# GpSimd computes the low halves of its weights in operations of 256 columns instead of 1024

## The chip, the cores and the metric

The kernel runs on one core of one Trainium2 chip. The core has five engines with queues of their own: TensorE (PE in the rows; its weight loads are listed apart as PEld), VectorE (DVE), ScalarE (ACT), GpSimd (POOL) and SyncE (SP, which here only issues transfers). Each engine takes its instructions in a fixed order, and waits between engines are semaphores. The metric is device time in microseconds (us), lower is better; it is the median of three runs.

## The reference, cut to what matters

Two transformer-like blocks run on 256 positions of width 2048, all in float32. The first has attention, a pooling branch and a feed-forward part with a short convolution; the second works on 272 positions (16 more in front) and has a state-space scan with a second, 31-tap convolution, and then a neighbourhood attention. Nearly all arithmetic is in products of activations with large weight matrices:

```python
proj = h @ w_in[l]                                        # 2048 x 4096
x = x + jnp.concatenate([a, m], axis=-1) @ w_out[l]       # 2048 x 2048
u = h @ w_up                                              # 2048 x 11264
return (jax.nn.silu(gate) * val) @ w_down                 # 5632 x 2048
proj = jnp.einsum("bld,de->ble", u, w_in)                 # even layer: 2048 x 12352
h + jnp.einsum("ble,ed->bld", jnp.concatenate([y_a, y_b], axis=-1), w_out)   # 4096 x 2048
proj = jnp.einsum("bld,de->ble", u, w_in)                 # odd layer: 2048 x 8192
```

## The kernel before

**Products in three parts.** To keep float32 accuracy with TensorE's faster fp32r operands, every operand is split into a high part, which is the value rounded to fp32r, and a low part, which is the value minus the high part. A product is then three matmuls per 128 rows of depth: `wh*xh` (L226), `wh*xl` (L227) and `wl*xh` (L228), all added in one PSUM tile `acc`. The function is `products`; `rows` (L239 to L241) is a variant with the operands' roles exchanged, used for the first block's q, k and v.

**Chunks and pieces.** Weights come in chunks of 128 output columns, in the order that `plan` writes down: a `raw` tile of 128 partitions by up to 2048 columns, that is, 16 blocks of depth 128 side by side. Three `raw` buffers are loaded ahead by SP (L165). `split_next` splits a chunk in pieces of 8 blocks (1024 columns). For each piece ScalarE writes the high part, `wH` (L185), and VectorE or GpSimd subtracts it from the weights to get the low part, `wL` (L186). Both have four buffers, so two chunks. A chunk of the feed-forward's second matrix (`down`) has 11 blocks: one piece of 1024 columns and one of 384.

**Who splits.** The table `POOL` names for each kind of chunk how many of its pieces go to GpSimd: one of two for most, both for `B`, `C` and `xs` (the inputs of the scan), none for `k` and `q` but one piece of each of the first chunks. VectorE does the rest. `chunk` calls `split_next` for the next chunk before the current chunk's matmuls are written, so a chunk is split while the one before it is multiplied. The first three chunks are already split in operations of a quarter piece (`step = n // 4`, 256 columns).

**What else these engines do.** VectorE takes the products out of PSUM, adds and scales, splits activations (`split_act`, `xl` at L265 and L268), does the convolutions' taps (L666, L770, with a PSUM tile as input and output), and the scan's element-wise work (`e`, `A`, `z`, `u`: L857, L865, L866, L810, L914). ScalarE does the high parts, activations and copies out of PSUM. GpSimd does little but its low parts.

**The order** on each engine is that of the program text, as the tile framework lays it out. The places spoken of below: the mixing step of the pooling branch (`pooled`, `mix`; about 164 to 227 us from the span's start), the scan (`meta_set`, `heads`, `pair`; 1460 to 1660 us), and the second half of the even layer's output projection (chunks `e_out` with half 0; 1810 to 1916 us). In that last loop each of the 16 outputs `t` is scaled, added and reordered on VectorE (L1006 to L1009), stored by ScalarE's queue (L357), and split for the next layer (L267, L268).

Of the kernel before, what the change touches and what calls it, by code (L numbers as in the profile page):

```python
# [10 lines left out]
F32 = mybir.dt.float32  # L11
F32R = mybir.dt.float32r
AF = mybir.ActivationFunctionType
OP = mybir.AluOpType
# [43 lines left out]
class Kernel:  # L58
# [112 lines left out]
    def split_next(self):  # L171

        nc = self.nc
        key = self.order[self.n_split][0]
        raw, kt, pieces = self.wt[self.n_split]
        k0 = len(pieces) * self.PIECE
        n = min(self.PIECE, kt - k0) * P
        w = raw[:, k0 * P:k0 * P + n]
        H = self.wp.tile([P, self.PIECE * P], F32R, name="wH", tag="wH", bufs=self.PIECES)
        L = self.wp.tile([P, self.PIECE * P], F32R, name="wL", tag="wL", bufs=self.PIECES)  # L180
        eng = nc.gpsimd if self.on_pool(key, len(pieces)) else nc.vector
        step = n // 4 if self.n_split < 3 else n
        for o in range(0, n, step):
            c = slice(o, o + step)
            nc.scalar.activation(H[:, c], w[:, c], AF.Copy)  # L185
            eng.tensor_tensor(L[:, c], w[:, c], H[:, c].bitcast(F32), op=OP.subtract)  # L186
        pieces.append((H, L))
        if k0 * P + n == kt * P:
            self.n_split += 1
# [1080 lines left out]
```

## Time and profile before

| what | us |
|---|---|
| median of 3 runs | 2448.98 (2447.66 to 2449.26) |
| profiled execution, its own time | 2449.59 |
| its span, first to last instruction | 2447.8 |
| PE busy in it | 2410.7 (98%) |
| DVE busy | 1639.5 (67%) |
| ACT busy | 1308.1 (53%) |
| POOL busy | 1046.8 (43%) |

A busy time is the union of an engine's instructions. The mean of one matmul (286 ns) is its length from entry to end; as matmuls overlap, one enters every 0.12 us. "Idle before" is the time that an engine stood still before an instruction, with the instruction that let it go on. The span is cut into windows where a stage is of interest; PEclk in a window is the share of TensorE's full clock that was granted in it.

### The profile page before, as it was taken

What the parts mean: (1) busy time and instruction counts of PE and PEld (TensorE: products, weight loads), DVE (VectorE), ACT (ScalarE), POOL (GpSimd) and SP (SyncE); (2) the same over time, 40 slices, a digit from 0 to 9 for tenths busy, and PEclk for the clock granted to TensorE, in tenths of its full rate; (3) what the DMA queues carried; (4) which work ended last, traced back from release to release, by engine and by line L of the source; (5) the groups of instructions that cost most, each with busy time, mean ns of one, the idle gap of its engine ahead of it and who ended that gap; (6) DMA issues with size and microseconds to landing.
All of it is one profiled execution on the core that took longest, in us unless ns stands there. A gap on an engine that the chain in (4) does not pass through costs nothing.

```text
span 2447.8 us, 48352 instructions
## 1 busy us (share of the span) xinstructions
PE 2410.7 (98%) x19718; PEld 2373.6 (97%) x19718; DVE 1639.5 (67%) x2770; ACT 1308.1 (53%) x2125; POOL 1046.8 (43%) x441
## 2 busy tenths in 40 slices
PE   8999999999999999999999999999999999999998
PEld 8998999999999999999999998889999999999998
DVE  6566456666666666779999988798767544444433
ACT  6564455554454454553547766775544444445553
POOL 1133444445445545654458863323434333333443
PEclk9999999999999999999999999999999999999999
DMA  8545655556756756875455555555676544445553
GB/s 283 184 146 181 235 193 184 188 184 205 234 188 200 243 181 197 256 230 180 163 193 187 189 169 198 180 181 168 224 236 203 183 159 172 158 171 182 187 190 121
DMA packets 116415, 471.47 MB, mean 193 GB/s; under 512 B 17376, under 2 KB 54496, under 8 KB 72416
## 3 DMA queue, kind: packets, MB, share of 16 engines
q1 hardware_dynamic: 94880, 443.87, 53.6%
q10 hardware_dynamic: 21312, 24.52, 2.8%
q8 instruction: 154, 2.52, 0.4%
q14 instruction: 69, 0.57, 0.1%
HBM read 448.79 MB, written 19.54 MB: 191 GB/s over the span
## 4 chain that ended last, share of the span: by engine, by line
PE 90%; DVE 3%; issue 2%; ACT 2%; DMA 1%; SPq 0%; POOL 0%; ACTq 0%; POOLq 0%; DVEq 0%
PE acc L226 27%; PE acc L227 27%; PE acc L228 27%; PE acc L241 2%; PE acc L239 2%; PE acc L240 2%; ACT wH L185 1%; PE cvp L1078 1%; PE gp L1068 1%; DVE wL L186 1%; DVE win L513 1%; PE gp L1044 1%; PE cvp L888 0%; DVE e L865 0%; ACT e L849 0%
## 5 line engine op out<-in xcount | busy, mean ns | idle before, releaser
L226 PE MATMUL acc<-xh,wH 128*128 128x256 f32 (+1 forms) x5856 | 1675.1, 286 | 9.4 <-ACT xh L267 6.2
L227 PE MATMUL acc<-xl,wH 128*128 128x256 f32 (+1 forms) x5856 | 1670.4, 285 | 0.0
L228 PE MATMUL acc<-xh,wL 128*128 128x256 f32 (+1 forms) x5856 | 1667.2, 285 | 0.4
L186 POOL TENSOR_TENSOR wL<-raw,wH 128x1024 fp32r<-128x1024 f32 (+1 forms) x435 | 1042.5, 2399 | 1382.3 <-ACT wH L185 1282.5
L185 ACT ACTIVATE wH<-raw 128x1024 fp32r<-128x1024 f32 (+1 forms) x838 | 832.0, 998 | 790.8 <-PE acc L227 589.4
L226 PEld LDWEIGHTS acc<-xh,wH 128*128 128x128 f32 x5856 | 1108.5, 189 | 17.6 <-ACT xh L267 6.6
L228 PEld LDWEIGHTS acc<-xh,wL 128*128 128x128 f32 x5856 | 1107.7, 189 | 1.5 <-POOL wL L186 1.0
L227 PEld LDWEIGHTS acc<-xl,wH 128*128 128x128 f32 x5856 | 1107.6, 189 | 1.5 <-issue 0.8
L186 DVE TENSOR_TENSOR wL<-raw,wH 128x1024 fp32r<-128x1024 f32 (+2 forms) x403 | 582.0, 1446 | 144.4 <-ACT wH L185 139.0
L666 DVE SCALAR_TENSOR_TENSOR cvp<-u,prm,cvp 128x264 f32<-128x264 f32 (+14 forms) x480 | 211.0, 489 | 1.4 <-ACT cvp L660 0.7
L265 DVE TENSOR_TENSOR xl<-y,xh 128x256 fp32r<-128x256 f32 x44 | 98.7, 2243 | 25.1 <-ACT xh L264 25.1
L239 PE MATMUL acc<-wH,xh 128*128 128x256 f32 x384 | 109.2, 286 | 6.0 <-ACT xh L267 6.0
L590 DVE TENSOR_TENSOR u<-acc,r 128x256 f32<-128x256 f32 x88 | 36.7, 418 | 110.6 <-PE acc L228 108.5
L241 PE MATMUL acc<-wH,xl 128*128 128x256 f32 x384 | 109.0, 285 | 0.7 <-DVE xl L268 0.6
L240 PE MATMUL acc<-wL,xh 128*128 128x256 f32 x384 | 107.9, 283 | 0.0
L239 PEld LDWEIGHTS acc<-wH,xh 128*128 128x128 f32 x384 | 73.1, 191 | 6.2 <-ACT xh L267 6.1
L291 DVE TENSOR_TENSOR nacc<-nacc,sq 128x272 f32<-128x272 f32 (+1 forms) x103 | 68.2, 662 | 10.4 <-ACT sq L280 9.2
L241 PEld LDWEIGHTS acc<-wH,xl 128*128 128x128 f32 x384 | 73.2, 191 | 1.6 <-DVE xl L268 1.5
L240 PEld LDWEIGHTS acc<-wL,xh 128*128 128x128 f32 x384 | 72.9, 191 | 0.1
L770 DVE SCALAR_TENSOR_TENSOR gp<-c,prm,gp 128x270 f32<-128x270 f32 (+1 forms) x128 | 63.8, 498 | 5.7 <-ACT gp L766 5.3
L622 DVE TENSOR_TENSOR xw<-acc,xw 128x256 f32<-128x256 f32 x64 | 27.2, 425 | 51.6 <-PE acc L228 48.2
L592 ACT ACTIVATE y<-u,prm 128x256 f32<-128x256 f32 x88 | 52.2, 594 | 14.9 <-DVE u L590 14.7
(227 smaller groups left out, 1416.5 us busy)
## 6 DMA issues: line engine op xcount, KB each, us to landing
raw<-in_e_w_in_dram SPq DMA_DIRECT2D x97, 1024.0 KB
raw<-in_w_up_dram SPq DMA_DIRECT2D x88, 1024.0 KB
raw<-in_o_w_in_dram SPq DMA_DIRECT2D x64, 1024.0 KB
raw<-in_w_down_dram SPq DMA_DIRECT2D x64, 704.0 KB
raw<-in_e_w_out_dram SPq DMA_DIRECT2D x32, 1024.0 KB
raw<-in_w_qkv_dram SPq DMA_DIRECT2D x21, 1024.0 KB
raw<-in_w_out_dram SPq DMA_DIRECT2D x16, 1024.0 KB
raw<-in_o_w_out_dram SPq DMA_DIRECT2D x16, 1024.0 KB
```

The costliest lines, as they stand in the source:

```text
L185: nc.scalar.activation(H[:, c], w[:, c], AF.Copy)
L186: eng.tensor_tensor(L[:, c], w[:, c], H[:, c].bitcast(F32), op=OP.subtract)
L226: nc.tensor.matmul(ps, wh, xh, start=k == 0, stop=False)
L227: nc.tensor.matmul(ps, wh, xl, start=False, stop=False)
L228: nc.tensor.matmul(ps, wl, xh, start=False, stop=k == n - 1)
L239: nc.tensor.matmul(ps[b], xh, H[:, o:o + 256], start=k == 0, stop=False)
L240: nc.tensor.matmul(ps[b], xh, L[:, o:o + 256], start=False, stop=False)
L241: nc.tensor.matmul(ps[b], xl, H[:, o:o + 256], start=False, stop=k == 15)
L265: nc.vector.tensor_tensor(l, x, h.bitcast(F32), op=OP.subtract)
L291: nc.vector.tensor_tensor(st["acc"], st["acc"], sq, op=OP.add)
L666: nc.vector.scalar_tensor_tensor(cps[i][:, a:b], u[i][:, a + s:b + s], self.prm_("dww", k * 16 + i), cps[i][:, a:b], op0=OP.mult, op1=OP.add)
L770: nc.vector.scalar_tensor_tensor(y[:, a:b], t[:, a + d:b + d], self.prm_("ecw", k * 32 + c), y[:, a:b], op0=OP.mult, op1=OP.add)
```

## The change

The subtraction that makes `wL` is written in operations of at most 256 columns where GpSimd does it. Where VectorE does it, and in ScalarE's `wH`, nothing is changed.

```diff
         eng = nc.gpsimd if self.on_pool(key, len(pieces)) else nc.vector
         step = n // 4 if self.n_split < 3 else n
+
+        sub = 256 if eng is nc.gpsimd else step
         for o in range(0, n, step):
             c = slice(o, o + step)
             nc.scalar.activation(H[:, c], w[:, c], AF.Copy)
-            eng.tensor_tensor(L[:, c], w[:, c], H[:, c].bitcast(F32), op=OP.subtract)
+            for i in range(o, o + step, sub):
+                c = slice(i, min(i + sub, o + step))
+                eng.tensor_tensor(L[:, c], w[:, c], H[:, c].bitcast(F32), op=OP.subtract)
```

GpSimd's 427 operations of 1024 columns become 1708 of 256; its 8 operations of the first chunks are as they were. On the other four engines no instruction is moved, added or removed. What stands differently is what they wait for. GpSimd's queue in the second half of the output projection (`e_out`), before:

```order
L186 TENSOR_TENSOR wL<-raw,wH 128x1024 [waits DMAHW3_49,PE_49,Activation_49]
L186 TENSOR_TENSOR wL<-raw,wH 128x1024 [waits DMAHW6_49,PE_49,Activation_49]
L186 TENSOR_TENSOR wL<-raw,wH 128x1024 [waits DMAHW1_49,PE_49,Activation_49]
L186 TENSOR_TENSOR wL<-raw,wH 128x1024 [waits DMAHW4_49,PE_49,Activation_49]
L186 TENSOR_TENSOR wL<-raw,wH 128x1024 [waits DMAHW7_49,PE_49,Activation_49]
```

GpSimd's queue there, with the change (L190 is L186 of before):

```order
L190 TENSOR_TENSOR wL<-raw,wH 128x256 [waits DMAHW3_49,PE_49,Activation_49]
L190 TENSOR_TENSOR wL<-raw,wH 128x256 x3
L190 TENSOR_TENSOR wL<-raw,wH 128x256 [waits DMAHW6_49,PE_49,Activation_49]
L190 TENSOR_TENSOR wL<-raw,wH 128x256 x3
L190 TENSOR_TENSOR wL<-raw,wH 128x256 [waits DMAHW1_49,PE_49,Activation_49]
L190 TENSOR_TENSOR wL<-raw,wH 128x256 x3
```

Each piece is now four operations; the first carries the waits (for the load, for TensorE to be done with the buffer, and for ScalarE's high part), and the three behind it carry none.

TensorE's queue at a chunk of the same stage, the first piece, before:

```order
L226 MATMUL acc<-xh,wH 128x272 [waits Activation_49]
L227 MATMUL acc<-xl,wH 128x272
L228 MATMUL acc<-xh,wL 128x272 [waits Pool_49]
L226 MATMUL acc<-xh,wH 128x272
L227 MATMUL acc<-xl,wH 128x272
L228 MATMUL acc<-xh,wL 128x272
L226 MATMUL acc<-xh,wH 128x272
L227 MATMUL acc<-xl,wH 128x272
L228 MATMUL acc<-xh,wL 128x272
```

TensorE's queue there, with the change (L230 to L232 are L226 to L228 of before):

```order
L230 MATMUL acc<-xh,wH 128x272 [waits Activation_49]
L231 MATMUL acc<-xl,wH 128x272
L232 MATMUL acc<-xh,wL 128x272 [waits Pool_49]
L230 MATMUL acc<-xh,wH 128x272
L231 MATMUL acc<-xl,wH 128x272
L232 MATMUL acc<-xh,wL 128x272
L230 MATMUL acc<-xh,wH 128x272
L231 MATMUL acc<-xl,wH 128x272
L232 MATMUL acc<-xh,wL 128x272 [waits Pool_49]
```

The matmuls stand where they stood. Each quarter of a GpSimd piece now has a wait of its own, in front of every second `wl*xh` matmul, where one wait for the whole piece stood at its first; that is 1277 waits more.

## Rows read from the trace of the kernel before

**Rows 1.** The page's first part: busy time of each engine over the span.
```profile
PE 2410.7 (98%) x19718; PEld 2373.6 (97%) x19718; DVE 1639.5 (67%) x2770; ACT 1308.1 (53%) x2125; POOL 1046.8 (43%) x441
```

**Rows 2.** PE's waits, 190 to 230 us: for whom, us in total, times, longest.
```profile
PE acc L226 <- ACT xh L267: 2.9, 1, 2.9
PE acc L226 <- DVE xl L268: 2.6, 2, 2.1
```

**Rows 3.** PE's waits, 1400 to 1700 us.
```profile
PE gp L817 <- DVE mu L905: 4.4, 1, 4.4
PE cvp L894 <- DVE xl L265: 4.0, 3, 3.2
```

**Rows 4.** PE's waits, 1900 to 1920 us.
```profile
PE acc L226 <- ACT xh L267: 3.4, 1, 3.4
```

**Rows 5.** Windows: length, busy PE, PEld, DVE, ACT, POOL, then PEclk, DMA, GB/s.
```profile
198.50:205.30 6.80, 5.08 (x24) 5.08 (x25) 4.92 (x13) 1.90 (x4) 0.47 (x1) 0.50 0.27 77
...
1478.50:1482.00 3.50, 3.50 (x15) 2.69 (x16) 3.50 (x10) 2.14 (x6) 0.00 (x0) 0.51 0.51 157
1557.00:1563.80 6.80, 6.41 (x23) 5.58 (x24) 3.69 (x9) 4.27 (x9) 0.00 (x0) 0.50 0.87 294
1642.40:1645.80 3.40, 3.40 (x17) 3.40 (x16) 3.40 (x3) 1.16 (x2) 2.84 (x1) 0.50 0.88 304
...
1915.40:1922.20 6.80, 6.01 (x23) 5.53 (x24) 4.59 (x5) 2.85 (x4) 2.36 (x1) 0.50 0.69 194
```

**Rows 6.** Line L186, both engines: count, shortest/median/longest in ns, first and last start.
```profile
L186 POOL TENSOR_TENSOR wL<-raw,wH x435: 755/2402/4750, 9.8 to 2422.9; 128x1024 fp32r<-128x1024 f32 x142, 128x256 fp32r<-128x256 f32 x3
L186 DVE TENSOR_TENSOR wL<-raw,wH x403: 409/1225/2893, 5.1 to 2425.6; 128x1024 fp32r<-128x1024 f32 x107, 128x384 fp32r<-128x384 f32 x22, 128x256 fp32r<-128x256 f32 x6
```

**Rows 7.** Timeline, one turn of the `e_out` loop: start, us, engine, line, operation, [idle before].
```profile
1883.78 0.52 ACT L267 ACTIVATE xh<-xw,prm 128x272 fp32r<-128x272 f32 x1 [3.62 <-DVE xw L1009]
...
1885.65 2.62 POOL L186 TENSOR_TENSOR wL<-raw,wH 128x1024 fp32r<-128x1024 f32 x1 [3.76 <-ACT wH L185]
...
1886.55 2.81 DVE L186 TENSOR_TENSOR wL<-raw,wH 128x1024 fp32r<-128x1024 f32 x1 [0.54 <-ACT wH L185]
...
1889.36 0.39 DVE L1009 COPY xw<-eo 128x256 f32<-128x256 f32 x1
...
1890.18 0.52 ACT L267 ACTIVATE xh<-xw,prm 128x272 fp32r<-128x272 f32 x1 [3.66 <-DVE xw L1009]
```

**Rows 8.** Timeline of DVE in the pooling branch: two held operations and a free one.
```profile
170.90 2.38 DVE L520 TENSOR_TENSOR mix<-mix,p 128x16 f32<-128x16 f32 x1
...
192.93 0.42 DVE L513 TENSOR_TENSOR win<-win 128x252 f32<-128x252 f32 x1
...
197.11 2.14 DVE L513 TENSOR_TENSOR win<-p 128x255 f32<-128x255 f32 x1
```

**Rows 9.** Timeline, operations of GpSimd back to back, and a DVE operation among them.
```profile
1268.05 7.36 POOL L186 TENSOR_TENSOR wL<-raw,wH 128x1024 fp32r<-128x1024 f32 x3
...
1270.70 2.44 DVE L745 TENSOR_TENSOR u<-u,sig 128x272 f32<-128x272 f32 x1
```

**Rows 10.** Timeline of the first chunks: four 256-column operations on GpSimd, DVE beside them.
```profile
15.47 3.59 POOL L186 TENSOR_TENSOR wL<-raw,wH 128x256 fp32r<-128x256 f32 x4 [2.31 <-ACT wH L185]
...
17.51 1.82 DVE L268 SCALAR_TENSOR_TENSOR xl<-xin,prm,xh 128x256 fp32r<-128x256 f32 x2
```

**Rows 11.** Timeline in the scan: one kind of DVE operation free and held, GpSimd's beside it.
```profile
1545.89 1.49 DVE L914 TENSOR_TENSOR u<-u,r 128x272 f32<-128x272 f32 x4
...
1546.16 4.75 POOL L186 TENSOR_TENSOR wL<-raw,wH 128x1024 fp32r<-128x1024 f32 x1 [6.85 <-ACT wH L185]
...
1548.91 5.90 DVE L914 TENSOR_TENSOR u<-u,r 128x272 f32<-128x272 f32 x5
```

**Rows 12.** Window in the stage with both pieces on GpSimd; columns as in rows 5.
```profile
1300.00:1400.00 100.00, 100.00 (x800) 99.78 (x799) 91.56 (x226) 78.06 (x116) 81.24 (x35) 1.00 0.54 187
```

**Rows 13.** The page's groups: weight loads of `wL`, busy, mean ns, idle before.
```profile
L228 PEld LDWEIGHTS acc<-xh,wL 128*128 128x128 f32 x5856 | 1107.7, 189 | 1.5 <-POOL wL L186 1.0
```

## The prediction

> **What bounds the kernel now.** I read the busy times first: PE is busy for 2410.7 of the span's 2447.8 us, POOL for 1046.8 [rows 1]. POOL's own length is therefore not the question. What the change can reach is where PE stands still, or runs at half its clock after it stood still, and what it must not do is to make POOL late for PE.
>
> PE's waits gather in three places. In the mixing step of the pooling branch PE waits 2.9 us for `xh` and 2.6 us for `xl` [rows 2]; in the scan 4.4 us for `mu` and 4.0 us for `xl`, both from DVE [rows 3]; at the end of the first half of `e_out`'s second loop 3.4 us for `xh` [rows 4]. After each, a window has the granted clock at 0.50, the lower level of 1.2 GHz [rows 5]. What PE did there at half speed is lost by half: 5.08 / 2 = 2.5 us after the mixing step, (3.50 + 6.41 + 3.40) / 2 = 6.7 us in the scan, 6.01 / 2 = 3.0 us after `e_out`. Together 2.9 + 2.6 + 2.5 = 8.0, 4.4 + 4.0 + 6.7 = 15.1 and 3.4 + 3.0 = 6.4 us, that is 29.5 us.
>
> Then I asked why DVE is late at these places, and the timelines answer. DVE's low part of 1024 columns takes 1.22 us in the middle, 2.89 at most [rows 6]. In each turn of the `e_out` loop it takes 2.81 us: it starts 0.90 us after a POOL operation of 2.62 us, and ends 1.09 us behind that one's end, about its own length [rows 7]. So it does nothing until POOL is done: it is held. The same shows in the pooling branch, where an operation on 128x16 takes 2.38 us, and one on 255 columns 2.14 us, where its free sister needs 0.42 [rows 8], and in the scan, where four `u` operations take 1.49 us when free and five take 5.90 beside POOL [rows 11]. All these DVE operations read two SBUF tiles. It goes the other way too: POOL's 4.75 us [rows 11] contain the time in which DVE's run of `u` operations stood ahead of it.
>
> **The change, part by part.**
>
> *A piece on POOL gets longer.* One of 1024 columns takes 2.40 us in the middle, one of 256 columns 0.755 at the shortest [rows 6]. Four make 3.02 us if nothing disturbs them, 3.59 where DVE got between them [rows 10]. I take 3.02, since in the stage where it matters (below) DVE has few such operations, and keep 3.59 for the range. The 427 pieces cost POOL 427 x 0.62 = 265 us, which by itself is free: POOL is idle for 57% of the span.
>
> *Where POOL has both pieces* (`B`, `C`, `xs`; 32 chunks, 64 pieces) it is 81% busy, and PE does 800 matmuls in 100 us [rows 12], 0.125 us each, so a piece's 24 matmuls take 3.00 us. A piece of 3.02 is behind by 0.02 x 64 = 1.3 us over the stage. Against that stands what the finer waits give: a quarter releases its own two blocks, so PE can begin on a piece 2.40 - 0.755 = 1.64 us earlier than now. 1.64 is over 1.3: I cost this at nothing. The cover is gone above 3.00 + 1.64 / 64 = 3.03 us a piece.
>
> *PE's 1277 new waits.* The weight loads of `wL` carry the old ones; 5856 of them show 1.5 us of idle time before them in all [rows 13]. If every new wait cost what these loads cost on average, 1277 x 1.5 / 5856 = 0.3 us. I take 0; above, 0.3; below zero there is nothing to win, since nothing waits there.
>
> *The hold gets shorter.* A DVE operation that comes while POOL works now waits for the rest of an operation of up to 2.40 us, afterwards for the rest of one of 0.755, if DVE gets its turn between two POOL operations. It does: three POOL operations back to back last 7.36 us, and DVE's `u` (L745), which started within the second, took 2.44 us and so ended before the third was over [rows 9]; among the 256-column operations of the first chunks two DVE operations take 0.91 us each [rows 10], not the rest of the piece. Against the trace stands a rule of the Trainium skill: GPSIMD Engine Reference, 2.1 Instruction dispatch, says that the completion of an operation does not hold back the next Pool instruction, and that each of GpSimd's cores goes on to it as soon as its share is done. By that rule a gap between quarters need not exist, and the sum below would turn into the third rival's; the rows just named show a turn at the seam, so I go by them.
>
> - `e_out`: the turn is 1890.18 - 1883.78 = 6.40 us [rows 7], against PE's 48 matmuls x 0.125 = 6.00. DVE's `wL` is in the chain of that turn, directly ahead of `xw` (L1009) and `xh` [rows 7]. It arrives 0.90 us into the piece, so in the second quarter, and waits until 2 x 0.755 = 1.51: held 0.61 instead of 2.62 - 0.90 = 1.72. The turn would be 6.40 - 1.11 = 5.29 us, under PE's 6.00. PE becomes the bound of this loop, and 0.40 us saved per turn would already do. Gain: the whole 6.4 us (bounds 0 and 6.4).
> - The mixing step: five holds lie in its chain, from the first to the third row of [rows 8], together about 9.65 us over free durations (2.38 and 2.14 are the first and the last). At one quarter each, 5 x 0.755 = 3.8 stay, so up to 5.9 us of the chain go. But DVE runs almost without gaps there, and may meet two quarters of one piece. I take 5 of the 8.0 us (bounds 0 and 8.0).
> - The scan: the five `u` operations of [rows 11] are held 5.90 - 5 x 0.37 = 4.0 us by two pieces; with quarters 1.5 stay, so 2.5 go, from the wait of 4.0 or from its half clock. I put the same 2.5 on the wait of 4.4, whose chain has two POOL pieces beside it too, and 1.0 on the last window of half clock. That is 6 of 15.1 us (bounds 0 and 15.1); the rest is DVE's and ACT's own work.
>
> Sum: 6.4 + 5 + 6 = 17.4 us off the profiled execution's 2449.59, that is 2432.2. The profiled time is 0.6 above the median of 2448.98, so I say **2432**.
>
> **The rivals.**
>
> 1. *Holds are shared out anew.* Between two DVE operations of a run POOL gets its next quarter, so a run of four meets four holds of 0.755, 3.0 us in place of 2.0. The two slow operations in a row at 17.51 [rows 10] speak for this; against it speaks the run of four free ones ahead of POOL's late one [rows 11]. Then mixing and scan give nothing, and in `e_out` the copy L1009 meets the third quarter: 1.11 - 0.755 = 0.36 of the 0.40 us per turn are won, some 4 us of 6.4 at most. That is 2445.6 or more; about **2447**, no change that could be told.
> 2. *POOL becomes the bound in `B`, `C`, `xs`* (slower). At 3.59 us a piece, PE would wait 64 x (3.59 - 3.00) - 1.6 = 36 us; with the 17.4 us won elsewhere that is 2449.6 - 17.4 + 36 = **2468**. It costs from 3.03 us a piece, and decides the sign from 3.00 + (17.4 + 1.6) / 64 = 3.30. For it: 3.59 is the only row of four quarters in a row. Against it: DVE's operations beside those four read two SBUF tiles at each output, those in this stage mostly come from PSUM.
> 3. *GpSimd does not let go between quarters* (slower). A hold is then up to 3.02 us in place of 2.40. `e_out`: 15 turns x 0.62 = 9.3 us more; mixing 5 x 0.62 = 3.1; scan 4 x 0.62 = 2.5: 2449.6 + 14.9 = **2464.5**. This is the time by the page named above; [rows 9, 10] speak against it.
> 4. *All of it goes.* PE finds its operands ready at all three places: 2449.6 - 29.5 = **2420**. Against it: the scan's chains hold much work of DVE and ACT that no POOL operation touches.
>
> That the change does not do what it says is excluded: the order shows four operations for one, and the waits by quarter.
>
> **How the numbers follow.** Forecast (2424 to 2441) 0.54; all of it goes 0.16; shared out anew 0.16; POOL the bound 0.08; never lets go 0.06. A measurement of this kernel can tell a difference of about 0.2%, 4.9 us. So: faster 0.54 + 0.16 = 0.70, the same 0.16, slower 0.14. The range takes in the forecast's bounds, all of the fourth rival and most of the first: 2418 to 2449; the slower cases stay outside it.
>
> **What would show it.** In the `e_out` loop DVE's `wL` at about 1.8 us instead of 2.81, the turn at 6.0, and PE's wait of 3.4 us with the half clock behind it gone: right for `e_out`. The 255-column operations of the mixing step at 0.4 to 1.2 us, and waits there below 3 us: right for the holds. POOL's 256-column operations at 0.70 to 0.76 us and no wait of PE for POOL between 1265 and 1455 us: right for the stage with both pieces. Wrong would be: DVE's `wL` in `e_out` above 2.8 us (third rival); PE waiting for `wL` of POOL again and again while both pieces are POOL's (second); as many us of held DVE operations in the mixing step and the scan as now, in smaller portions (first).

## The result, and the profile after

The changed kernel takes 2417.15 us (median; 2416.74 to 2419.06) against 2449.12 for the kernel before beside it: a ratio of 0.9871, with a 95% interval of 0.9857 to 0.9886. That is 32 us faster, where 17 were forecast, and it lies 0.9 us below the range.

The profiled execution took 2416.97 us, its span 2415.2. The first row of its page answers to [rows 1]; the second is GpSimd's low parts and the third the weight loads of `wL` (as [rows 13]; line, operation, count, busy us, mean ns, idle before).

```profile
PE 2396.5 (99%) x19718; PEld 2363.3 (98%) x19718; DVE 1464.8 (61%) x2770; ACT 1304.1 (54%) x2125; POOL 1340.5 (56%) x1722
...
L190 POOL TENSOR_TENSOR wL<-raw,wH 128x256 fp32r<-128x256 f32 x1716 | 1336.2, 810 | 1056.4 <-ACT wH L187 1046.4
...
L232 PEld LDWEIGHTS acc<-xh,wL 128*128 128x128 f32 x5856 | 1103.2, 188 | 0.2
```

POOL is busy for 294 us more than before and nobody is late for it: the loads of `wL`, with 1277 waits more, show 0.2 us of idle time in all. DVE, whose instructions are the same, is busy for 175 us less. That is time in which it stood held with an operation begun.

PE's waits in the changed kernel, over the whole span (us in total, times, longest), which answer to [rows 2 to 4]:

```profile
PE acc L243 <- ACT xh L271: 5.8, 1, 5.8
PE cvp L898 <- DVE xl L269: 0.8, 2, 0.6
PE acc L230 <- DVE xl L272: 0.8, 1, 0.8
PE gp L342 <- ACT rs L335: 0.7, 1, 0.7
PE acc L245 <- DVE xl L272: 0.6, 1, 0.6
PE acc L230 <- ACT xh L271: 0.5, 1, 0.5
PE gp L821 <- DVE mu L909: 0.2, 1, 0.2
PE gp L330 <- ACT sq L284: 0.2, 1, 0.2
```

The first is the kernel's very start, which has nothing to do with the change. The wait of 4.4 us for `mu` is 0.2, the 4.0 for `xl` in the scan 0.8, the 3.4 at the end of `e_out` is gone. With them went the half clock: these windows lie where those of [rows 5] lay (same columns; PEclk is the number after POOL's).

```profile
198.00:205.00 7.00, 7.00 (x62) 7.00 (x61) 4.12 (x7) 2.72 (x4) 2.81 (x4) 1.00 0.45 152
...
1466.00:1473.00 7.00, 7.00 (x58) 7.00 (x58) 7.00 (x16) 4.26 (x9) 3.28 (x4) 1.00 0.57 193
1538.00:1545.00 7.00, 7.00 (x54) 6.23 (x51) 3.72 (x8) 5.13 (x10) 4.60 (x4) 1.00 0.74 236
1886.00:1893.00 7.00, 7.00 (x56) 6.92 (x56) 4.97 (x6) 3.47 (x5) 5.08 (x6) 1.00 0.63 189
```

PE runs the same matmuls in the same order in both kernels, so the start of one matmul in the two traces tells where the time went:

| stage | start of the same matmul before, after (us) | ahead | won in the stage |
|---|---|---|---|
| ahead of the mixing step's waits | 194.1, 193.4 | 0.7 | 0.7 |
| behind the mixing step | 226.9, 218.9 | 8.0 | 7.3 |
| ahead of the scan's first wait | 1455.0, 1446.6 | 8.4 | 0.4 |
| behind the scan | 1651.8, 1626.9 | 25.0 | 16.6 |
| behind `e_out` | 1921.2, 1889.0 | 32.2 | 7.2 |
| end of the span | 2447.8, 2415.2 | 32.6 | 0.4 |

The three places that the prediction named give 31.1 of the 32.6 us; what was wrong is how much each gives. The 0.7 us of the first row are there at 20 us already and are not the change's: the traces of the eleven other kernels whose first three chunks are split alike stand there between 0.2 us behind the kernel before and 1.1 ahead of it. A difference of two traces below 1 us says little.

### The profile page after: what moved, and what is told of

It is laid out like the page before. It is cut to its first block, busy times and chain, and to the rows that moved or that the text cites. A ratio compares the mean times of both kernels' runs of the same rounds, so it can differ in the third digit from the quotient of the medians.

```text
span 2415.2 us, 49918 instructions
## 1 busy us (share of the span) xinstructions
PE 2396.5 (99%) x19718; PEld 2363.3 (98%) x19718; DVE 1464.8 (61%) x2770; ACT 1304.1 (54%) x2125; POOL 1340.5 (56%) x1722
## 4 chain that ended last, share of the span: by engine, by line
PE 96%; DVE 1%; issue 1%; ACT 1%; DMA 1%; POOL 0%; SPq 0%; POOLq 0%; ACTq 0%
PE acc L230 29%; PE acc L231 29%; PE acc L232 29%; PE acc L245 2%; PE acc L243 2%; PE acc L244 2%; PE cvp L1082 1%; PE gp L1072 1%; PE gp L1048 1%; PE cvp L892 0%; PE cvp L898 0%; DVE e L870 0%; PE gp L1042 0%; ACT wH L187 0%; POOL wL L190 0%
## 5 line engine op out<-in xcount | busy, mean ns | idle before, releaser
L190 POOL TENSOR_TENSOR wL<-raw,wH 128x256 fp32r<-128x256 f32 x1716 | 1336.2, 810 | 1056.4 <-ACT wH L187 1046.4
L230 PE MATMUL acc<-xh,wH 128*128 128x256 f32 (+1 forms) x5856 | 1670.1, 285 | 1.3 <-DVE xl L272 0.8
L232 PE MATMUL acc<-xh,wL 128*128 128x256 f32 (+1 forms) x5856 | 1662.6, 284 | 0.0
L230 PEld LDWEIGHTS acc<-xh,wH 128*128 128x128 f32 x5856 | 1104.0, 189 | 9.0 <-issue 3.3
L232 PEld LDWEIGHTS acc<-xh,wL 128*128 128x128 f32 x5856 | 1103.2, 188 | 0.2
L190 DVE TENSOR_TENSOR wL<-raw,wH 128x1024 fp32r<-128x1024 f32 (+2 forms) x403 | 477.5, 1187 | 154.9 <-ACT wH L187 145.8
L295 DVE TENSOR_TENSOR nacc<-nacc,sq 128x272 f32<-128x272 f32 (+1 forms) x103 | 57.8, 561 | 12.4 <-ACT sq L284 10.7
L853 ACT ACTIVATE e<-A,sbT 128x128 f32<-128x128 f32 (+2 forms) x160 | 53.3, 375 | 5.8 <-DVE A L861 2.6
L271 ACT ACTIVATE xh<-xw,prm 128x272 fp32r<-128x272 f32 (+1 forms) x48 | 24.6, 513 | 51.7 <-DVE xw L1013 46.3
```

Source lines behind the costliest of these rows:

```text
L230: nc.tensor.matmul(ps, wh, xh, start=k == 0, stop=False)
L232: nc.tensor.matmul(ps, wl, xh, start=False, stop=k == n - 1)
L295: nc.vector.tensor_tensor(st["acc"], st["acc"], sq, op=OP.add)
L853: nc.scalar.activation(to, A4[:, d, i, l:l + n], AF.Exp, bias=sbT[:, c, h:h + 1])
```

## The experiments

Each kernel is the changed one with one edit; each time is a median with the ratio to the kernel before beside it.

**Is it the shorter hold, or the finer release to TensorE?** Both came with one edit. Here only the hold is short:

```diff
-            for i in range(o, o + step, sub):
+            for i in reversed(range(o, o + step, sub)):
```

> The changed kernel with the quarters of each GpSimd piece written last one first, so TensorE's first wL matmul of a piece waits for the whole piece, as before the change. Theory (the gain is shorter holds of VectorE): the holds are those of the changed kernel, so 2417 to 2421 us; up to 3 us more where both pieces are GpSimd's, since a piece of 4 x 0.69 us is whole only some 0.4 us later than one of 2.40. Rival (the gain is the finer release of wL to TensorE): the gain is gone, 2447 to 2452.

2419.08 us, ratio 0.9878 (0.9863 to 0.9893). The gain stays when a piece is released as a whole, as before the change. PE's wait for `mu` did not come back, nor that at the end of `e_out`, and PE shows no wait for GpSimd; the loads of `wL` stood idle for 0.3 us on its account in all. The finer release is not the cause.

**One place at a time.** The edit names the chunks in which GpSimd splits by 256 columns, for instance:

```diff
-        sub = 256 if eng is nc.gpsimd else step
+        sub = 256 if eng is nc.gpsimd and key[0] in ("e_out", "oq", "ok", "ov") else step
```

> GpSimd splits in 256 columns only in the chunks e_out, oq, ok and ov, in 1024 elsewhere. Theory (three places, each with its own holds): only the e_out term comes, 7 us by the comparison of the two traces, so 2442 us, and the waits in the mixing step and the scan are those of before (5.5 and 8.4 us and more). Rival (a common cause, such as GpSimd's shorter operations everywhere): well under or over that, with the other two waits changed.

2441.40 us, 0.9969 (0.9958 to 0.9981): 7.4 us won, 7 expected.

> GpSimd splits in 256 columns only in the chunks p, pool and w_out. Theory: only the mixing step's term, 8 us, so 2441 us; the five holds there are cut to a quarter each. The prediction's own size of this term was 5 us, 2444.

2442.07 us, 0.9974 (0.9964 to 0.9983): 6.7 us won, and 6.9 by the starts of its matmuls in its trace, from 194 to 227 us of the kernel before (the 8 us of the expectation had the scatter of the kernel's start in it). Both are above the prediction's 5; the interval, 4.2 to 8.8 us, does not exclude it.

> GpSimd splits in 256 columns only in the chunks z_a and z_b, which are split during the scan. Theory (VectorE has a backlog without a gap from about 1440 us on, so each hold since then counts, and the last xs pieces at 1444 and 1447 us hold it too, by 0.98 and 1.15 us more than in the changed kernel): the first wait of the scan comes down but stays at 1 to 3 us, the other two go; 13 to 15 of the 17 us, 2434 to 2436. Rival (only the two pieces right beside each wait count, as the prediction's step had it): 6 us with a wait for mu near 2 us and one for xl above 1.5, 2443.

2434.65 us, 0.9943 (0.9928 to 0.9957): 14.2 us won, as the theory of a backlog had it, and not the 6 of the prediction's step. PE's waits for DVE in the scan of this kernel, and the window right at the first of them:

```profile
PE cvp L898 <- DVE xl L269: 1.6, 3, 0.6
PE gp L821 <- DVE mu L909: 1.6, 1, 1.6
...
1474.00:1477.40 3.40, 3.16 (x24) 2.75 (x25) 3.40 (x8) 1.94 (x5) 0.76 (x2) 1.00 0.64 158
```

1.6 us of the wait for `mu` are left, and behind it the granted clock is 1.00. So a wait need not go to nothing for all of its half clock to come back.

**Where does the rest of the scan's gain come from?** The last `xs` pieces are split before the scan's first wait, from 1438 to 1447 us of the kernel before. First all `xs` chunks were added to `z_a` and `z_b`:

> GpSimd splits in 256 columns only in the chunks xs, z_a and z_b. Theory (the backlog reaches back into the last xs pieces): the whole 17 us of the scan, 2432, and 1 to 4 us less than with z_a and z_b alone. Rival (only pieces split beside the waits count): the same as with z_a and z_b alone.

2438.34 us, 0.9959 (0.9944 to 0.9974): 3.7 us slower than with `z_a` and `z_b` alone, which neither theory had. The timelines (start, us) of DVE and of GpSimd in this kernel say why:

```profile
1443.91 5.87 DVE L861 TENSOR_TENSOR A<-A,cc 128x512 f32<-128x512 f32 x1
1450.40 0.68 DVE L861 TENSOR_TENSOR A<-A,cc 128x512 f32<-128x512 f32 x1
...
1434.54 14.69 POOL L190 TENSOR_TENSOR wL<-raw,wH 128x256 fp32r<-128x256 f32 x21
```

The two DVE rows are the same operation; free, it takes 0.68 us. The first one was held for 5.2 us, until GpSimd's row of 21 quarters ended at 1449.23, through seven whole ones that followed one another at 14.69 / 21 = 0.70 us without a gap. Here GpSimd did not let go between quarters. A copy at 1397 us was held for 3.9 us in the same way. Two kernels tell whether splitting `xs` is at fault, or these stretches are:

> 256 columns in B, C, xs, z_a and z_b. With xs, z_a and z_b alone VectorE was shut out of two stretches, 4.0 and 5.9 us, through 5 and 7 quarters without a turn between them, and the time was 2438 in place of 2432. In the changed kernel that does not show. Theory A (it is B and C being split too that makes the difference): no such stretch, 2431 to 2433. Theory B (whether VectorE gets its turn in a long unbroken run of quarters is a matter of chance or of alignment): one or more such stretches here too, 2434 to 2440.

2431.22 us, 0.9926 (0.9911 to 0.9941). No such stretch in its trace, although more chunks are split.

> 256 columns in z_a, z_b and the last two xs chunks only, 16 quarters before the first z_a piece. Theory (holds in VectorE's backlog ahead of the scan count, and the loss with all xs chunks came from the two stretches in which VectorE was shut out in long runs): the hold of the two A operations near 1445 us is a quarter each, the wait for mu goes below 1 us, 2431 to 2434. Rival (splitting xs at all costs time): 2436 or more. Rival (those holds don't count): 2434.7, as with z_a and z_b alone.

2432.02 us, 0.9930 (0.9914 to 0.9947): 2.6 us more than with `z_a` and `z_b` alone, from 16 operations ahead of the scan. PE's waits from 1400 to 1720 us are then down to this:

```profile
PE cvp L898 <- DVE xl L269: 0.8, 2, 0.6
PE gp L821 <- DVE mu L909: 0.2, 1, 0.2
```

Why these 16 operations count is in DVE's timeline of the kernel before (first three rows) and of the changed one (last four). They are the same instructions, some 25 to 30 us ahead of the wait for `mu`:

```profile
1445.27 1.94 DVE L857 TENSOR_TENSOR A<-A,cc 128x512 f32<-128x512 f32 x1
1447.83 2.36 DVE L857 TENSOR_TENSOR A<-A,cc 128x512 f32<-128x512 f32 x1
1451.27 2.21 DVE L801 TENSOR_SCALAR z<-z,sb 128x272 f32<-128x272 f32 x1
```

```profile
1436.88 0.96 DVE L861 TENSOR_TENSOR A<-A,cc 128x512 f32<-128x512 f32 x1
1438.48 1.21 DVE L861 TENSOR_TENSOR A<-A,cc 128x512 f32<-128x512 f32 x1
1440.78 0.37 DVE L805 TENSOR_SCALAR z<-z,sb 128x272 f32<-128x272 f32 x1
...
1443.12 2.25 DVE L813 COPY z<-c 128x32 f32<-128x32 f32 x4
```

The three together are 3.97 us shorter; the copies in the last row give 1.83 back (2.25 us for four that take 0.42 when free). What is left is not lost again. In the kernel before DVE does stand idle three times between here and the wait for `mu`, each time for ACT (1.86, 2.77 and 1.51 us). But ahead of the first and the third ACT had been waiting for DVE, as its timeline in the kernel before shows (in brackets the idle time before, and who ended it), and ahead of the second it had worked without a gap since the first of these rows:

```profile
1454.51 1.28 ACT L773 ACT_TABLE_LOAD   x1 [3.08 <-DVE gp L770]
...
1470.56 1.28 ACT L773 ACT_TABLE_LOAD   x1 [2.32 <-DVE z L811]
```

So the chain that ends in the wait for `mu` goes back from DVE to ACT and to DVE again. How far the same DVE instruction is ahead in the changed kernel, beyond the 8.4 us by which PE is ahead in front of the scan, by its starts in the two traces:

| DVE instruction (start before) | ahead by |
|---|---|
| first `A` (1445.27) | 0.0 us |
| `z` (1451.27) | 2.1 |
| behind the copies, `c` (1454.90) | 1.2 |
| `wL` (1463.86) | 2.9 |
| behind `z`, L810 (1469.69) | 4.6 |
| `mu` (1477.90) | 5.6 |

The first of ACT's waits above ends with DVE's `gp` (1453.94), which is 3.9 us ahead and stands in front of the copies; ACT's own next operation is 3.3 ahead. What the copies take back on DVE does not delay ACT.

The two waits that PE has there, for `c` and for `mu`, were 1.2 and 4.4 us (the second in [rows 3]), together 5.6; 0.2 is left.

**Do the three places add up, and is anything left for the rest?**

> GpSimd in 256 columns in the chunks of all three places (p, pool, w_out; z_a, z_b; e_out, oq, ok, ov), in 1024 elsewhere. Theory (three separate places, and VectorE's backlog ahead of the scan adds what is left): the three single gains add up, 7.4 + 6.7 + 14.2 = 28.3 us, 2420.5; the changed kernel's other 3 us come from holds ahead of the scan, so a wait for mu of 1 to 2 us stays. Rival (operations of 256 columns help or hurt everywhere a little): 2417 or below, or above 2424.

2419.73 us, 0.9881 (0.9866 to 0.9896): 30.0 us against a sum of 28.3 of the three kernels. A wait of 1.6 us for `mu` stayed, as expected.

> GpSimd in operations of 256 columns in the chunks of the three places and the last two xs chunks, 1024 elsewhere. Theory: the 2 to 3 us that the three places lacked were the holds ahead of the scan; with them the whole gain of the changed kernel, 2416 to 2418, with a wait for mu below 1 us. Rival (the rest of the chunks gives something too): 2419 to 2421.

2418.01 us, 0.9877 (0.9862 to 0.9891), with 0.2 us for `mu`. With 16 operations more than the three places have, the whole gain of the changed kernel is there; splitting the rest is worth nothing that can be told. The time alone does not tell this kernel from the one with the three places, as the intervals overlap; the wait for `mu` does, with 0.2 us in place of 1.6.

**How long may an operation be?**

> GpSimd in operations of 512 columns, two a piece, everywhere. Theory: an operation of about 1.25 us holds VectorE by at most that. In e_out VectorE's wL comes 0.9 us into the piece, waits 0.35, and the whole 7 us come; in the mixing step and the scan the holds are halved: if the gain goes with the length of an operation, 32 x (2.40 - 1.25) / (2.40 - 0.70) = 22 us, 2427; if the waits end as soon as VectorE has caught up, all of it, 2418. So 2418 to 2428. Rival (only the finer release counts): e_out gives nothing.

2438.62 us, 0.9964 (0.9952 to 0.9977): 10 us won, about half of the least that the expectation's range had. By the starts of its matmuls the mixing step gave 3.1 and the scan 8.1 us, about half of the changed kernel's, and `e_out` almost nothing: the wait at its end is 3.6 us. The groups of the little copy L1008 (now L1012) between 1815 and 1905 us, free in the kernel before, then in this one, then in the changed one; and one turn of this kernel's timeline:

```profile
L1008 DVE COPY xw<-eo 128x16 f32<-128x16 f32 x14 | 2.3, 162 | 0.0
```

```profile
L1012 DVE COPY xw<-eo 128x16 f32<-128x16 f32 x14 | 15.4, 1098 | 0.0
...
1874.91 1.70 DVE L190 TENSOR_TENSOR wL<-raw,wH 128x1024 fp32r<-128x1024 f32 x1 [0.54 <-ACT wH L187]
1876.54 1.26 DVE L1012 COPY xw<-eo 128x16 f32<-128x16 f32 x1
...
1881.28 1.70 DVE L190 TENSOR_TENSOR wL<-raw,wH 128x1024 fp32r<-128x1024 f32 x1 [0.54 <-ACT wH L187]
```

```profile
L1012 DVE COPY xw<-eo 128x16 f32<-128x16 f32 x12 | 8.4, 703 | 0.0
```

DVE's `wL` is let in after the first half, and is 1.1 us shorter than in [rows 7]. Then GpSimd's second half goes ahead of the copy behind it, which takes 1.26 us in place of 0.16. The turn is 1881.28 - 1874.91 = 6.37 us, as before. The hold was handed on to the next operation. With quarters the same happens, but the copy takes 0.70, and the turn falls below PE's own 6.00 us.

> GpSimd in operations of 128 columns, eight a piece. From 0.69 us start to start for 256 columns and 2.40 us for 1024, one of 128 should take 0.42 us, a piece 3.3 us. Theory (a piece above 3.03 us makes GpSimd the bound where it has both pieces, 64 of them): 64 x 0.33 - 2 = 19 us of new waits for wL there, 2436 us, the holds as short as or shorter than with 256 columns. Rival (what binds there is not the length of a piece): 2414 to 2418.

2450.99 us, 1.0003 (0.9991 to 1.0016). Its runs spread from 2443.0 to 2456.4 us, and the profiled one is the shortest of them. In its trace the window with both pieces on GpSimd (as [rows 12]) has POOL busy throughout and 723 matmuls in place of 800:

```profile
1300.00:1400.00 100.00, 99.45 (x723) 98.47 (x722) 80.60 (x196) 70.13 (x103) 100.00 (x236) 1.00 0.47 161
```

236 operations in 100 us are 0.42 us each, 3.4 a piece, above PE's 3.00. In the same 100 us PE does 723 / 24 = 30.1 pieces, so it goes at GpSimd's pace. Hardly any of it shows as idle time: the weight loads stand idle for `wL` for 1.6 us in the whole stage, the rest does not show as waits of its own. By the starts of its matmuls PE enters the stage 7.9 us ahead of the kernel before and leaves it 8.6 behind: 16.5 us lost, 19 expected. This trace has a shut-out too, an `A` operation of 12.57 us at 1452. What makes the other runs of this kernel longer isn't known: they have no trace.

The same size only at the three places and the last two `xs` chunks:

> GpSimd in operations of 128 columns, but only in the chunks of the three places and the last two xs chunks; 1024 elsewhere. Theory (what 128 columns lost everywhere was the stage with both pieces on GpSimd, and the gain ends where TensorE no longer waits): as much as with 256 columns, 2416 to 2419, although a hold is then a quarter of a microsecond shorter still. Rival (shorter holds give more still): 2414 or below. Rival (eight operations a piece cost in other ways): above 2421.

2422.25 us, 0.9894 (0.9878 to 0.9911), 3 us above the expected range and 4 above the same chunks in 256 columns. They are one more shut-out, again of the `A` operation (0.68 us when free):

```profile
1436.48 6.99 DVE L861 TENSOR_TENSOR A<-A,cc 128x512 f32<-128x512 f32 x1
...
PE gp L821 <- DVE mu L909: 3.2, 1, 3.2
```

The wait for `mu` is back at 3.2 us. In the mixing step, in the scan from 1500 us on and in `e_out` its matmuls gain at most 1 us on those of the changed kernel: little is left to win once PE does not wait. No kernel tried is faster than the changed one.

## Why the prediction was wrong

The mechanism was right: VectorE is held by GpSimd's operations at three places, a shorter operation holds it for less, and PE's waits and its half clock behind them go. Two terms of the sum were too small, that of the mixing step and above all that of the scan. Term by term:

- *A piece on GpSimd*: 3.02 us forecast. Operations of 256 columns follow each other at 0.70 us, so a piece takes 2.8. The durations overlap, and four of them are not their sum. This cost the forecast nothing, but it is why the second rival was never near: in a window of the stage with both pieces GpSimd is busy for 93.6%, and PE does 800 matmuls in 100 us as before:

```profile
1300.00:1400.00 100.00, 100.00 (x800) 99.78 (x799) 90.26 (x220) 76.45 (x113) 93.63 (x133) 1.00 0.53 182
```

- *PE's 1277 new waits*: 0 forecast, and 0.
- *`e_out`*: 6.4 forecast, 7.2 by the two traces, 7.4 alone. The size was right, its working not quite. The turn was to fall by 1.11 us; `wL` and the copy together fell from 2.81 + 0.16 to 1.57 + 0.70 us, so by 0.70 (a turn of the changed kernel):

```profile
1852.50 1.57 DVE L190 TENSOR_TENSOR wL<-raw,wH 128x1024 fp32r<-128x1024 f32 x1
1853.99 0.70 DVE L1012 COPY xw<-eo 128x16 f32<-128x16 f32 x1
1854.61 0.38 DVE L1013 COPY xw<-eo 128x256 f32<-128x256 f32 x1
...
1858.48 1.58 DVE L190 TENSOR_TENSOR wL<-raw,wH 128x1024 fp32r<-128x1024 f32 x1
```

  The first rival's mechanism is in this row: the copy now meets a quarter and takes 0.54 us longer. But 0.70 us a turn are left, more than the 0.40 that were needed. The turn is now 5.98 us, which is PE's.
- *The mixing step*: 5 forecast, 7.3 measured by the traces, of 8.0 in sight. The step left one quarter at each of five holds. In the changed kernel three of the five operations are not held at all (170.90 of [rows 8], 2.38 us, takes 0.17), because DVE, once early, meets GpSimd at other moments. That is luck that the step could not count on: the first of the three now starts 0.07 us ahead of GpSimd's piece, before 0.02 us behind it. Others are held in their place, by 0.54 us at most. All of DVE's operations from the first of the five to the fifth add up to 22.3 us, before to 28.3: 6.0 less, where the step had up to 5.9. What it missed is what follows from that: PE's waits there fell from 6.0 us (0.5 of them for `p`, which the sum left out) to 1.3, and the half clock of 2.5 came back whole.
- *The scan*: 6 forecast, 16.6 measured by the traces. This is the step that failed: it put 2.5 us on each wait, for the two pieces beside it, and called the rest DVE's and ACT's own work. DVE and ACT take turns in being late there, and so every hold in that chain counted, back to 30 us ahead of the wait: the lead grows from 0.0 to 5.6 us in the table above. PE's waits in the scan fell from 10.8 us to 1.0, and the half clock of 6.7 went with them, 16.5 together. The run of five `u` operations gave what was forecast (5.90 us to 3.63), but it was the last of several. Leaving out the pieces at the front shows it: by the starts of the matmuls the scan gains 13.6 us with `z_a` and `z_b` alone, 16.6 with the last two `xs` chunks as well.
- *The half clock* was treated as if it came back in parts. After a wait of 1.6 us in one kernel the clock stood at 1.00; with 512 columns, after 2.8 us, a window shows 0.57:

```profile
1471.00:1475.00 4.00, 3.28 (x14) 2.48 (x15) 4.00 (x11) 2.27 (x6) 0.00 (x0) 0.57 0.36 70
```

- *The bound*: the fourth rival, with 2420, was the one that came, and the low end of the range rested on its 29.5 us. That sum left out two waits of the scan put down to ACT, for `c` and `cb`, of 1.2 us each. ACT was behind DVE there, and both went too. The argument against this rival, that much of the scan's chains is work that no GpSimd operation touches, overlooked that this work starts as late as the held operations ahead of it let it.

The third rival was given 0.06 from the rows with turns at the seam. In the changed kernel it doesn't show. In three other kernels GpSimd does not let go between operations, at one or two operations of DVE in each. The Trainium skill, GPSIMD Engine Reference, 2.1 Instruction dispatch, has the next operation begin on each GpSimd core without waiting for the whole of the last. That a core is always reading in these stretches would fit it; no run here shows the cores one by one.

## What to carry to other kernels

Where an engine holds another one, follow the chain of a wait back until an engine in it was early, and count every hold on the way, however far ahead of the wait: an idle time that ends with an engine that was itself late does not end the chain. A hold made shorter is partly handed on to the operation behind, so add up the row of operations, not the one that was seen held. Cut the holding engine's work no finer than its own bound allows, at the stage where it has the least room.

## What was not expected of the hardware

A GpSimd operation on two SBUF operands takes 2.40 us with 1024 columns; those of 256 and 128 columns follow each other at 0.70 and 0.42 us, so cutting a piece in four costs some 0.4 us, in eight 1.0.

Between two of GpSimd's operations VectorE nearly always gets its turn, and then each of them alternates with the other, one operation each. But four times in the traces of all these kernels VectorE stood held through 5 to 28 operations: for 4.04 and 5.87 us with all of `xs` in quarters (5 and 7 operations), for 12.57 and 6.99 us with 128 columns (28 and 15). Three of the four are the same operation (`A`, two SBUF inputs, 512 columns), which in the changed kernel and in four others with quarters there took 0.95 or 0.96 us. All four came in an unbroken row of GpSimd operations, and three of them ended only with that row (at 1401.11, 1449.23 and 1442.92 us); the longest ended 3 us before its row did. But there were longer rows without any. What decides it stays open; that the changed kernel is spared is luck, as far as is known.

Not only operations with two SBUF inputs are held, which are all that the prediction named. Of the rows above, the copies of `xw` and of `z` read one tile each, and the `z` operation L801 one tile and a column of scalars; it took 2.21 us beside GpSimd, and 0.37 in the changed kernel.
